# A scaled copy bound by its transfers: loads and stores in turns instead of side by side

## The chip, the cores and the metric

The kernel runs on one core of one Trainium2 chip. The metric is the device time of one execution in microseconds (us); lower is better. Engines are named as in the profile: DVE is VectorE, ACT is ScalarE, POOL is GpSimd, SP is SyncE. DVE and ACT do arithmetic here; SP and ACT also start DMA transfers, each through a queue of its own (q1 belongs to SP, q10 to ACT).

## The reference

Each of 16 x 1024 tokens has a row of 512 float32 numbers and two weights. The output holds the row twice, each copy multiplied by one of the token's weights. The expert indices are not used.

```python
batch, seq, hidden, n_experts = 16, 1024, 512, 8
k = 2
x_expanded = x[:, :, np.newaxis, :].repeat(k, axis=2)
weights = expert_weights[..., np.newaxis]
return (x_expanded * weights).astype(np.float32)
```

So 33.6 MB are read and 67.1 MB written.

## The kernel before, in words

The 16384 tokens are 128 partitions times 128 rows. They are cut into five tiles of 25 rows (row here: one token in each partition) and a rest of 3 rows. A tile's input is `x_tile` (two buffers in turn); its output is written into `o_ring`, which holds one tile's output of 25 rows and is used anew by each tile. The output is handled in two halves, rows 0 to 12 (13 rows, half A) and rows 13 to 24 (12 rows, half B). In each half DVE makes the products of the first 8 rows (9 in tile 0), four rows to an instruction, and ACT makes the others, one instruction for each output row of 512 numbers. Then SP issues the store of that half.

Loads are issued on ACT, stores on SP. Tile 0 is loaded in two pieces (9 and 16 rows), the others in one. The six loads of weights go first on SP's queue. The load of tile i+2 is issued when tile i has been multiplied, since it writes into tile i's buffer, and the rest `z_tile` is loaded with tile 2. The rest is multiplied and stored last. Nothing keeps loads and stores apart: a load goes as soon as its buffer is free, a store as soon as its half is multiplied, and a half is multiplied as soon as the store that read that half of `o_ring` before has landed. Each engine works through its own instructions in order; the semaphores between them are set by the framework from the data that they touch.

In the profile, L79 issues the loads of `x_tile`, L87 that of `z_tile`, L93 those of the weights, L106 is ACT's product, L116 DVE's product, L141 the store, and L76 a copy of one number that orders the load of the rest behind tile 0.

Of the kernel before, what the change touches and what calls it, by code (L numbers as in the profile page):

```python
# [1 line left out]

# [4 lines left out]


@with_exitstack
def kernel(  # L10
    ctx: ExitStack,
    tc: tile.TileContext,
    x: bass.AP,
    expert_indices: bass.AP,
    expert_weights: bass.AP,
    out: bass.AP,
):
    nc = tc.nc

    batch, seq, hidden = x.shape  # L20
    k = expert_weights.shape[-1]
    P = nc.NUM_PARTITIONS
    ntok = batch * seq
    assert ntok % P == 0
    A_TOTAL = ntok // P

    f32 = mybir.dt.float32
    row = k * hidden
    CH = 4


    groups = [25, 25, 25, 25, 25]
    TX = max(groups)
    LAST = 3
    FIRST = [9, 16]
    SHARES = [[9, 9], [8, 8]]
    assert sum(groups) + LAST == A_TOTAL

    xf = x.rearrange("b s h -> (b s) h")
    of = out.rearrange("b s k h -> (b s) (k h)")  # L40
    wf = expert_weights.rearrange("b s k -> (b s) k")

    w_pool = ctx.enter_context(tc.tile_pool(name="w_pool", bufs=1))
    x_pool = ctx.enter_context(tc.tile_pool(name="x_pool", bufs=2))
    o_pool = ctx.enter_context(tc.tile_pool(name="o_pool", bufs=1))

    w_tile = w_pool.tile([P, A_TOTAL * k], f32)
    o_ring = o_pool.tile([P, TX * row], f32)

    def rows(of_all, done, T):  # L50
        return of_all[done * P : (done + T) * P, :].rearrange(
            "(p a) n -> p (a n)", a=T
        )


    if LAST:
        z_pool = ctx.enter_context(tc.tile_pool(name="z_pool", bufs=1))
        z_tile = z_pool.tile([P, LAST * hidden], f32)

    tiles = []  # L60
    done = 0
    for n in groups:
        tiles.append((done, n))
        done += n

    loaded = []

    def load(i):
        if i >= len(tiles):
            return  # L70
        done, n = tiles[i]
        x_tile = x_pool.tile([P, TX * hidden], f32)
        src = rows(xf, done, n)
        steps = FIRST if i == 0 else [n]
        if i == 2 and LAST:
            nc.scalar.copy(out=z_tile[:, :1], in_=o_ring[:, TX * row - 1 :])  # L76
        for e, step in enumerate(steps):
            at = sum(steps[:e])
            nc.scalar.dma_start(  # L79
                out=x_tile[:, at * hidden : (at + step) * hidden],  # L80
                in_=src[:, at * hidden : (at + step) * hidden],
            )
            if i == 0 and e == 0:
                for g in range(len(tiles) + 1):
                    weights(g)
        if i == 2 and LAST:
            nc.scalar.dma_start(out=z_tile, in_=rows(xf, A_TOTAL - LAST, LAST))  # L87
        loaded.append(x_tile)


    def weights(e):
        at, n = tiles[e] if e < len(tiles) else (A_TOTAL - LAST, LAST)
        nc.sync.dma_start(  # L93
            out=w_tile[:, at * k : (at + n) * k], in_=rows(wf, at, n)
        )

    def product(engine, o_tile, t, x_in, c, m):

        o = t * row
        if engine is not None:  # L100
            for e in range(m * k):
                out_e = o_tile[:, o + e * hidden : o + (e + 1) * hidden]
                in_e = x_in[:, e // k * hidden : (e // k + 1) * hidden]
                w_e = w_tile[:, c + e : c + e + 1]
                if engine is nc.scalar or engine is nc.any and (c + e) % 3 == 2:
                    nc.scalar.mul(out=out_e, in_=in_e, mul=w_e)  # L106
                else:
                    nc.vector.tensor_scalar(
                        out=out_e,
                        in0=in_e,  # L110
                        scalar1=w_e,
                        scalar2=None,
                        op0=mybir.AluOpType.mult,
                    )
            return
        nc.vector.tensor_tensor(  # L116
            out=o_tile[:, o : o + m * row].rearrange(
                "p (t k h) -> p t k h", t=m, k=k
            ),
            in0=x_in[:, : m * hidden]  # L120
            .rearrange("p (t h) -> p t h", t=m)
            .unsqueeze(2)
            .to_broadcast([P, m, k, hidden]),
            in1=w_tile[:, c : c + m * k]
            .rearrange("p (t k) -> p t k", t=m)
            .unsqueeze(3)
            .to_broadcast([P, m, k, hidden]),
            op=mybir.AluOpType.mult,
        )

    def fill(o_tile, x_in, c, m, v):
        for t in range(0, v, CH):
            u = min(t + CH, v)
            product(None, o_tile, t, x_in[:, t * hidden : u * hidden], c + t * k, u - t)
        product(nc.scalar, o_tile, v, x_in[:, v * hidden :], c + v * k, m - v)

    def emit(src, dst, c, cuts, shares):
        for at, to, v in zip(cuts, cuts[1:], shares):
            o_tile = o_ring[:, at * row : to * row]
            fill(o_tile, src[:, at * hidden : to * hidden], c + at * k, to - at, v)  # L140
            nc.sync.dma_start(out=dst[:, at * row : to * row], in_=o_tile)  # L141

    for i in range(2):
        load(i)
    for i, (done, n) in enumerate(tiles):
        emit(loaded[i], rows(of, done, n), done * k, [0, 13, n], SHARES[min(i, 1)])
        load(i + 2)
    emit(
        z_tile,
        rows(of, A_TOTAL - LAST, LAST),  # L150
        (A_TOTAL - LAST) * k,
        [0, LAST],
        [LAST],
    )

# [1 line left out]
_INS = ['x', 'expert_indices', 'expert_weights']  # L157
_OUTS = [((16, 1024, 2, 512), 'float32')]


# [23 lines left out]
```

## Time and profile before

| | us |
|---|---|
| median of 3 runs | 239.59 (239.44 to 239.84) |
| profiled execution, its own time | 239.73 |
| its span, first to last instruction | 238.0 |
| DVE busy | 93.2 |
| ACT busy | 55.2 |
| POOL busy | 0.2 |

The span is what the profile's times count from; 1.73 us of the execution lie around it. The DMA figures of the profile are shares of the core's 16 DMA engines, so 100% means that all sixteen move data all the time. "To landing" is the time from the issue of a transfer until its semaphore says that all of it has arrived.

### The profile page before, as it was taken

The numbers are of one execution on the slowest core, as the hardware profiler recorded it, in microseconds if no ns is written. First come the engines' busy times: TensorE is split into PE (matmuls) and PEld (weight loads), VectorE is DVE, ScalarE is ACT, GpSimd is POOL, SyncE is SP. The second block draws the span as 40 slices with busy tenths as digits, with TensorE's granted clock in tenths as the row PEclk, the third lists the DMA queues.
The fourth block names the chain that finished last, engine by engine and source line by source line (L and its number), as shares of the span: only waits on it lengthen the run. The fifth ranks groups of instructions, "written<-read, shape, count | busy, mean of one in ns | idle before, by whom it ended". The sixth has DMA issues, their size and how long they took to land.

```text
span 238.0 us, 214 instructions
## 1 busy us (share of the span) xinstructions
DVE 93.2 (39%) x23; ACT 55.2 (23%) x88; POOL 0.2 (0%) x4
## 2 busy tenths in 40 slices
DVE  0599800000059193086005902920085292861300
ACT  0008800000054170081005302700080280800000
POOL 0000000000000000000000000000000000000000
DMA  6999999999999999999999999999999999999996
GB/s 252 445 415 493 475 415 414 415 386 457 430 406 397 434 439 456 458 430 415 405 435 484 430 434 434 413 405 431 490 430 448 417 397 423 457 448 438 438 397 264
DMA packets 3457, 100.80 MB, mean 424 GB/s; under 512 B 1152, under 2 KB 1152, under 8 KB 1280
## 3 DMA queue, kind: packets, MB, share of 16 engines
q1 hardware_dynamic: 2448, 67.24, 65.5%
q10 hardware_dynamic: 1008, 33.55, 33.1%
q14 instruction: 1, 0.01, 0.0%
HBM read 33.69 MB, written 67.11 MB: 424 GB/s over the span
## 4 chain that ended last, share of the span: by engine, by line
DMA 69%; DVE 16%; issue 5%; ACT 3%; ACTq 0%; DVEq 0%; SPq 0%
DMA out_dram<-o_ring 62%; DVE o_ring L116 16%; DMA x_tile<-in_x_dram 7%; ACT o_ring L106 2%; ACT L106 1%; ACTq L79 0%; DVEq L116 0%; SPq L141 0%; ACTq L106 0%
## 5 line engine op out<-in xcount | busy, mean ns | idle before, releaser
L116 DVE TENSOR_TENSOR o_ring<-x_tile,w_tile 128x4096 f32<-128x4096 f32 (+1 forms) x22 | 89.8, 4130 | 122.4 <-DMA out_dram<-o_ring 102.8
L106 ACT ACTIVATE o_ring<-x_tile,w_tile 128x512 f32<-128x512 f32 x86 | 53.7, 708 | 134.4 <-DMA out_dram<-o_ring 134.4
L116 DVE TENSOR_TENSOR o_ring<-z_tile,w_tile 128x3072 f32<-128x3072 f32 x1 | 3.4, 3359 | 7.0 <-DMA out_dram<-o_ring 7.0
L106 ACT ACT_TABLE_LOAD x1 | 1.3, 1283 | 18.8 <-DMA x_tile<-in_x_dram 18.8
L76 ACT COPY z_tile<-o_ring 128x1 f32<-128x1 f32 x1 | 0.2, 191 | 0.0
L168 POOL MEMSET const-bfloat16-1.0<- 128x1 bf16 x1 | 0.1, 102 | 0.0
L168 POOL MEMSET const-uint8-127<- 128x1 uint8 x1 | 0.1, 102 | 0.0
L168 POOL MEMSET const-float32-1.0<- 128x1 f32 x1 | 0.1, 99 | 0.0
L168 POOL MEMSET const-float32-0.0<- 128x1 f32 x1 | 0.1, 98 | 0.2 <-issue 0.2
## 6 DMA issues: line engine op xcount, KB each, us to landing
out_dram<-o_ring SPq DMA_DIRECT2D x5, 6656.0 KB, 32.7
out_dram<-o_ring SPq DMA_DIRECT2D x5, 6144.0 KB, 36.4
x_tile<-in_x_dram ACTq DMA_DIRECT2D x4, 6400.0 KB, 29.7
x_tile<-in_x_dram ACTq DMA_DIRECT2D x1, 4096.0 KB, 17.6
x_tile<-in_x_dram ACTq DMA_DIRECT2D x1, 2304.0 KB, 8.1
out_dram<-o_ring SPq DMA_DIRECT2D x1, 1536.0 KB, 14.6
z_tile<-in_x_dram ACTq DMA_DIRECT2D x1, 768.0 KB, 10.5
w_tile<-in_expert_weights_dram SPq DMA_DIRECT2D x5, 25.0 KB, 24.7
```

The source lines that it names most:

```text
L76: nc.scalar.copy(out=z_tile[:, :1], in_=o_ring[:, TX * row - 1 :])
L106: nc.scalar.mul(out=out_e, in_=in_e, mul=w_e)
L116: nc.vector.tensor_tensor(out=o_tile[:, o : o + m * row].rearrange("p (t k h) -> p t k h", t=m, k=k), in0=x_in[:, : m * hidden] .rearrange ...
L168: nc = _bacc.Bacc("TRN2", target_bir_lowering=False, num_devices=1)
```

## The change

Loads and stores are put into four turns: load tiles 0, 1, 2 and the rest; store tiles 0, 1 and the rest; load tiles 3 and 4; store tiles 2, 3 and 4. Two helpers make the turns out of copies of one or two numbers on POOL, which do no arithmetic that the output needs: a copy reads or writes what one side must have finished with and what the other side must wait for, and the framework's semaphores do the rest.

- `stores_wait(src)`: POOL copies two numbers out of the newly loaded tile into `hold`, then two numbers of `o_ring` (one in each half) into `hold`, and back. The stores of both halves come after that. It stands after the loads of tile 2 and of tile 4.
- `load_waits(dst, t)`: POOL copies a number of `o_ring`'s half B into `hold`, back (which must wait until the store of tile 1's half B has landed), and then into the tile that the load writes. It stands ahead of the load of tile 3.
- Something is left in the queue at each turn: tile 2 is loaded as 24 rows and 1 row and then the rest, and tile 4 as 21 and 4 rows, and the stores wait for the first piece only; the rest's store (3 rows) stands behind that of tile 1, and the load of tile 3 waits for tile 1's store only.

The rest is multiplied ahead of tile 2 into rows 10 to 12 of `o_ring`, no longer at the end. Only the weights of tile 0 stay on SP's queue; the others go in three DMAs on ACT's queue, behind the load of tile 1. In the built kernel ACT's queue has, ahead of the load of tile 3, one product of tile 2 that needs the landing of tile 1's half B; and the first DVE instruction of tile 2's half B (rows 17 to 20) waits for that same landing, while the second (rows 13 to 16) waits for POOL.

```diff
-    FIRST = [9, 16]
-    SHARES = [[9, 9], [8, 8]]
+    CUT = 13
+    STEPS = {0: [9, 16], 2: [24, 1], 4: [21, 4]}
...
+    def stores_wait(src):
+        held = o_ring[:, : CUT * row + 1 : CUT * row]
+        nc.gpsimd.tensor_copy(out=hold, in_=src[:, :2])
+        nc.gpsimd.tensor_copy(out=hold, in_=held)
+        nc.gpsimd.tensor_copy(out=held, in_=hold)
+
+    def load_waits(dst, t):
+        one = o_ring[:, t * row : t * row + 1]
+        nc.gpsimd.tensor_copy(out=hold[:, :1], in_=one)
+        nc.gpsimd.tensor_copy(out=one, in_=hold[:, :1])
+        nc.gpsimd.tensor_copy(out=dst[:, :1], in_=one)
+
+    load(0, 0)
+    weights(nc.sync, 0, 1)
+    load(0, 1)
+    load(1, 0)
+    weights(nc.scalar, 1, 3)
+    weights(nc.scalar, 3, 5)
+    nc.scalar.dma_start(
+        out=w_tile[:, (A_TOTAL - LAST) * k :], in_=rows(wf, A_TOTAL - LAST, LAST)
+    )
     for i, (done, n) in enumerate(tiles):
-        emit(loaded[i], rows(of, done, n), done * k, [0, 13, n], SHARES[min(i, 1)])
-        load(i + 2)
...
+        if i == 2:
+            at = CUT - LAST
+            product(None, o_ring, at, z_tile, (A_TOTAL - LAST) * k, LAST)
+            nc.sync.dma_start(
+                out=rows(of, A_TOTAL - LAST, LAST),
+                in_=o_ring[:, at * row : CUT * row],
+            )
+            load_waits(x_pair[1], CUT)
+            load(3, 0)
+            vector(src, c, 0, v)
+            vector(src, c, CUT, CUT + v)
+            scalar(src, c, CUT + v, n)
+            scalar(src, c, v, CUT)
+            load(4, 0)
+            nc.scalar.copy(
+                out=x_pair[0][:, STEPS[4][0] * hidden :][:, :1],
+                in_=o_ring[:, CUT * row - 1 : CUT * row],
+            )
+            load(4, 1)
+            stores_wait(x_pair[0])
+            store(dst, 0, CUT)
+            store(dst, CUT, n)
+            continue
+        for at, to in [(0, CUT), (CUT, n)]:
+            vector(src, c, at, at + v)
+            scalar(src, c, at + v, to)
+            if i > 0:
+                store(dst, at, to)
+        if i == 0:
+            nc.scalar.copy(out=z_tile[:, :1], in_=o_ring[:, TX * row - 1 :])
+            load(2, 0)
+            load(2, 1)
+            nc.scalar.dma_start(out=z_tile, in_=rows(xf, A_TOTAL - LAST, LAST))
+            stores_wait(x_pair[0])
+            store(dst, 0, CUT)
+            store(dst, CUT, n)
```

More of the change, by code (lines that the diff above doesn't have):

```diff
@@ L53, in rows @@
         )
-    if LAST:
-        z_pool = ctx.enter_context(tc.tile_pool(name="z_pool", bufs=1))
-        z_tile = z_pool.tile([P, LAST * hidden], f32)
     tiles = []
@@ L64, with load, weights @@
         done += n
[L66 to L94, printed above, removed]
+    def load(i, e):
+        at = sum(STEPS.get(i, groups[i : i + 1])[:e])
+        to = at + STEPS.get(i, groups[i : i + 1])[e]
+        part = slice(at * hidden, to * hidden)
+        nc.scalar.dma_start(out=x_pair[i % 2][:, part], in_=rows(xf, *tiles[i])[:, part])
+    def weights(engine, g, to):
+        at, n = tiles[g]
+        engine.dma_start(
+            out=w_tile[:, at * k : (at + (to - g) * n) * k].rearrange(
+                "p (g m) -> p g m", g=to - g
+            ),
+            in_=wf[at * P : (at + (to - g) * n) * P, :].rearrange(
+                "(g p a) n -> p g (a n)", g=to - g, p=P
+            ),
         )
@@ L129, in product @@
         )
[L131 to L141, printed above, removed]
@@ L143, with vector @@
-    for i in range(2):
-        load(i)
-    for i, (done, n) in enumerate(tiles):
-        emit(loaded[i], rows(of, done, n), done * k, [0, 13, n], SHARES[min(i, 1)])
-        load(i + 2)
[L148 to L154, printed above, removed]
+    def vector(src, c, at, to):
+        for t in range(at, to, CH):
+            u = min(t + CH, to)
+            product(
+                None, o_ring, t, src[:, t * hidden : u * hidden], c + t * k, u - t
+            )
@@ new lines @@
+    for i, (done, n) in enumerate(tiles):
+        src, dst, c = x_pair[i % 2], rows(of, done, n), done * k
+        v = 9 if i == 0 else 8
+        if i == 2:
+            at = CUT - LAST
+            product(
+                None, o_ring, at, z_tile, (A_TOTAL - LAST) * k, LAST
+            )
+            nc.sync.dma_start(
+                out=rows(of, A_TOTAL - LAST, LAST),
+                in_=o_ring[:, at * row : CUT * row],
+            )
+            load_waits(x_pair[1], CUT)
[8 more added lines that the diff above has]
+                in_=o_ring[:, CUT * row - 1 : CUT * row],
+            )
+            load(4, 1)
[16 more added lines that the diff above has]
+            store(dst, CUT, n)
```

10 lines of the change are left out of this document (9 added, 1 removed).

## The prediction

> **What bounds the kernel now.** I read the DMA queues first, then the stretches, then the chain.
>
> ```profile
> span 238.0 us, 214 instructions
> q1 hardware_dynamic: 2448, 67.24, 65.5%
> q10 hardware_dynamic: 1008, 33.55, 33.1%
> DMA 69%; DVE 16%; issue 5%; ACT 3%; ACTq 0%; DVEq 0%; SPq 0%
> ...
> core 0: us, DVE busy (x) ACT busy (x) POOL busy (x), PEclk, DMA share, GB/s
> 0.00:1.80 1.80, 0.00 (x0) 0.00 (x0) 0.20 (x4) 1.00 0.02 3
> 5.00:48.00 43.00, 19.73 (x6) 10.16 (x16) 0.00 (x0) 1.00 1.01 432
> 52.00:92.00 40.00, 17.52 (x4) 11.24 (x18) 0.00 (x0) 1.00 1.00 434
> 96.00:122.00 26.00, 8.76 (x2) 6.24 (x10) 0.00 (x0) 1.00 1.00 435
> 100.00:168.00 68.00, 26.28 (x6) 17.48 (x28) 0.00 (x0) 1.00 1.00 431
> 236.90:238.00 1.10, 0.00 (x0) 0.00 (x0) 0.00 (x0) 1.00 0.00 0
> ```
>
> The queues' packets take 65.5 + 33.1 = 98.6% of the time of all sixteen DMA engines. What is missing is 1.4% of 238.0, or 3.3 us, and 1.8 us of that lie before the first packet and 1.1 us behind the last. So 0.4 us of idle DMA time are left in the whole middle. The chain says 69% DMA and gives 16% to DVE, but DVE's time costs nothing as long as the queues stay full, and the DMA share stands at 1.00 in the stretches where DVE multiplies. The bound is the transfers.
>
> Next, are loads and stores slower side by side? These stretches must first be told apart:
>
> ```profile
> ## 3 DMA queue, kind: packets, MB, share of 16 engines
> q10 hardware_dynamic: 497, 18.50, 99.6%
> q1 hardware_dynamic: 497, 0.09, 1.1%
> ...
> q1 hardware_dynamic: 409, 18.31, 58.7%
> q10 hardware_dynamic: 263, 12.65, 40.7%
> ...
> 25.12 42.86 DMA out_dram<-o_ring
> ```
>
> The first pair of rows is the stretch from 5 to 48 us: only loads (q10), with the weights in q1. The first store, issued at 25.12, lands 42.86 us later, at 67.98: on q1 it stands behind the weights, whose small pieces pass one by one between the loads' large ones, so loads of tiles 0, 1, 2 and the rest are over at about 51 before a store moves. From 52 to 92 there are only stores (the next load is issued at 91.41, below). The second pair is 96 to 168: both mixed. The rates are 432 alone, 434 alone, 435 and 431 mixed. Mixing costs nothing that could be won: (1 - 431/434) of 68 us is 0.5 us, and with the 0.4 us of gaps 0.9 us is the most that turns can bring. And the first turn is there already; what is new is the second half.
>
> **The change part by part.** Durations that I need:
>
> ```profile
> out_dram<-o_ring SPq DMA_DIRECT2D x5, 6656.0 KB, 32.7
> out_dram<-o_ring SPq DMA_DIRECT2D x5, 6144.0 KB, 36.4
> x_tile<-in_x_dram ACTq DMA_DIRECT2D x4, 6400.0 KB, 29.7
> out_dram<-o_ring SPq DMA_DIRECT2D x1, 1536.0 KB, 14.6
> z_tile<-in_x_dram ACTq DMA_DIRECT2D x1, 768.0 KB, 10.5
> ...
> L141 SPq DMA_DIRECT2D out_dram<-o_ring x11: 332/333/348, 25.1 to 222.5; - x11
> ...
> L116 DVE TENSOR_TENSOR o_ring<-x_tile,w_tile 128x4096 f32<-128x4096 f32 x20 | 87.6, 4421 | 122.4 <-DMA out_dram<-o_ring 102.8 <-issue 10.7 <-DMA x_tile<-in_x_dram 8.9
> L106 ACT ACTIVATE o_ring<-x_tile,w_tile 128x512 f32<-128x512 f32 x86 | 53.7, 708 | 134.4 <-DMA out_dram<-o_ring 134.4
> L116 DVE TENSOR_TENSOR o_ring<-z_tile,w_tile 128x3072 f32<-128x3072 f32 x1 | 3.4, 3359 | 7.0 <-DMA out_dram<-o_ring 7.0
> L76 ACT COPY z_tile<-o_ring 128x1 f32<-128x1 f32 x1 | 0.2, 191 | 0.0
> L168 POOL MEMSET const-bfloat16-1.0<- 128x1 bf16 x1 | 0.1, 102 | 0.0
> ...
> 0.73 8.50 ACTq L79 DMA_DIRECT2D x_tile<-in_x_dram  x3
> 91.41 0.36 ACTq L79 DMA_DIRECT2D x_tile<-in_x_dram  x1
> ...
> 219.00 0.03 issue
> 219.03 0.05 DVEq L116
> 219.08 0.04 issue
> 219.12 3.36 DVE o_ring L116
> ```
>
> At 434 GB/s (KB are 1024 bytes) half A's store streams for 15.7 us, half B's for 14.5, the rest's for 3.6; at 432 a tile loads in 15.2, the rest in 1.8, four rows in 2.4. Three small times: issue to first packet on an idle queue is 1.1 us (issued at 0.73, nothing before 1.80); last packet to landing is 0.3 us (the last store, issued at 222.5, lands 14.6 later at 237.1, and nothing moves after 236.9); landing to start of the waiting instruction is 0.12 us (219.00 to 219.12).
>
> Bytes are the same: no change in transfer time. Five tiles of weights move from q1 to q10 behind tile 1. On q1 they took 1.1% of 43 us, 0.5 us; on q10 I take the same, from nothing to twice that. They are needed first at 67, by tile 1. Two loads are split in two, which adds eight pieces to each DMA engine for each split, at most 0.1 us.
>
> *Turn 1, loads to stores, at about 51 us.* SP's first store now waits for POOL, and all stores queue behind it. The wait ends with the landing of tile 2's 24 rows, when one row (0.6) and the rest (1.8), 2.4 us, are still to stream. The path beside it: landing 0.3, three POOL copies one behind the other, 1.1 to the first packet. That leaves 1.0 us for the copies. A copy is 0.10 (POOL's MEMSET) to 0.19 (ACT's COPY of one column) plus 0.12 for its wait, so three take 0.7 to 0.9 us. Covered, cost 0 (0.6 if a copy takes 0.5 with its wait). DVE is idle then: tile 0 is multiplied by 28.7, and tile 1 must wait for the first store.
>
> *Inside the stores' turns.* A half's products start when the store before last lands: 0.3 + 0.12 + two DVE instructions of 4.42 + 1.1 to the first packet is 10.4 us, beside a 14.5 us store of the other half. Covered by 4 us, as from 52 to 92 now. If that cover went, each us over it would be lost.
>
> *Turn 2, stores to loads, at about 112.* Stores of tiles 0 and 1 take 2 x (15.7 + 14.5) = 60.4 us from 51, and the rest's store goes to 115.4. ACT's load of tile 3 waits for POOL; behind it on ACT queue the other products of tile 2 and the load of tile 4. It is released by the landing of tile 1's half B; what covers it is the rest's store, 3.6 us. The path: landing 0.3, two POOL copies 0.6 (on ACT one product of 0.71 and its wait, beside them: 0.8), first packet 1.1, together 2.2. That would be covered. But the same landing releases a DVE instruction of 4.42 us (rows 17 to 20), which reads two tiles, and DVE is free at that moment: the rest's product (3.36) and two of 4.42 begin at 98 and end at about 110. So the two POOL copies start beside it. No instant of the trace has POOL beside a working DVE: its four MEMSETs are over before the first packet. The price of the second copy is therefore open between 0.19 and 4.42 + 0.19 us. I take the upper end: a forecast shouldn't spend an overlap that no row shows, where two engines are let go by one event, and the longer instruction is the nearest row for how long the shorter may be held. Then the path is 0.3 + 0.12 + 4.42 + 0.19 + 0.12 + 1.1 = 6.2 us against a cover of 3.6, and sixteen DMA engines stand idle for **2.6 us**. At the lower end it costs 0.
>
> The Trainium skill, "SBUF — State Buffer", section on engine ports, says that VectorE's second input comes through a read port shared with GpSimd, so that a VectorE instruction with two SBUF inputs and a GpSimd instruction that reads SBUF exclude each other for a whole instruction. No run here shows it yet; by it turn 2 would cost those 2.6 us, without it nothing.
>
> Who waits then: DVE's next instruction (rows 13 to 16) needs POOL's last copy, and was to start at that time anyway. ACT has 13 products left (13 x 0.71 = 9.2 us) ahead of tile 4's load, which is thus issued at about 127, while tile 3 streams until 133. Covered by some 5 us.
>
> *Turn 3, loads to stores, at about 148.* As turn 1: four rows (2.4 us) cover 0.3 + 0.9 + 1.1. DVE is idle (tile 2 is done by 122). Cost 0 to 0.2, taken as 0.
>
> *The end.* The rest's product and store leave the end, where the product (219.12 to 222.48) lay beside half B's store. The last transfer is now half B of 12 rows. No change.
>
> Sum against the profiled execution: 239.73 + 2.6 = 242.3. The median of the three runs stands 0.14 below that execution, so 242.2.
>
> **The rivals.** *Nothing is held (not slower).* POOL's copies pass beside DVE, and each turn is covered. It decides at turn 2: as long as load 3's first packet comes within 3.6 us of the last packet of tile 1's store, that is, copies within 2.2 us of the landing, nothing is lost. For it: the 2.2 us path in total above. Against: the one DVE instruction beside it. Time: 239.6, between 239.2 and 240.3 with the splits, the weights and a visible 0.2 to 0.5 at turns 1 and 3.
>
> *Turns bring something.* Separate directions save the 0.9 us bounded above: 238.7. Against it stand 432, 434 and 435. For it only the 0.4 us of gaps and a mean of 431 in the long mixed stretch.
>
> *Every turn shows.* POOL's copies, none of which the trace has, take some 0.7 us each with their waits, not 0.3. Then turns 1 and 3 each stick out by 3 x 0.4 = 1.2 us, less 0.1, and turn 2 stays covered: 241.8; with the hold at turn 2, 244.8.
>
> *The change doesn't do what it says.* Turn 1 is such a case already: loads came first anyhow, so the wait there changes nothing by itself. For tiles 3 and 4 the semaphores leave no way round.
>
> **How the numbers follow.** Hold at turn 2: 0.50, 242.2, its own range 241.6 to 242.9. Nothing held: 0.28. Turns bring something: 0.08. Every turn shows: 0.14. About 0.2%, 0.5 us, is what a measurement of this kernel can tell from no change. Of "nothing held" 0.20 fall within that, 0.05 above and 0.03 below. So faster 0.11, same 0.20, slower 0.69. For 8 in 10 the range must reach down to 239.3, into "nothing held", and up to 243.3, over the hold's own range with a little for turns 1 and 3.
>
> **What would show it.** In the trace after: POOL's third copy of the load's wait starts over 4 us after the store of tile 1's half B lands, at the end of a 4.42 us DVE instruction, and the DMA share has one hole of 2 to 3 us between 112 and 120. At about 51 and 148 no hole over 0.3 us. Stretches of pure loads and pure stores stay at 432 and 434. It is wrong if POOL's copies run while DVE works (time near 239.6), if holes stand at 51 and 148, or if a pure stretch runs above 436.

## The result: 1.6% slower, and the profile after

The changed kernel takes 243.42 us (median of 6 runs, 243.22 to 243.45) against 239.62 for the kernel before (6 runs, 239.44 to 239.84): a ratio of 1.0157, 95% interval 1.0144 to 1.0170. That is 3.80 us more. The forecast had 242.2, 2.6 us more, and 243.42 lies 0.12 us above the top of its range.

The page of the changed kernel, the rows that answer to those of before:

```profile
span 241.6 us, 235 instructions
DVE 93.1 (39%) x23; ACT 55.4 (23%) x89; POOL 10.2 (4%) x13
...
q1 hardware_dynamic: 1728, 67.14, 64.5%
q10 hardware_dynamic: 1984, 33.66, 33.0%
...
L141 POOL COPY hold<-o_ring 128x1 f32<-128x1 f32 x1 | 4.3, 4252 | 36.6 <-DVE o_ring L100 36.6
L142 POOL COPY o_ring<-hold 128x1 f32<-128x1 f32 x1 | 4.4, 4421 | 21.4 <-DMA out_dram<-o_ring 21.4
L135 POOL COPY hold<-o_ring 128x2 f32<-128x2 f32 x2 | 0.4, 186 | 0.1
```

The queues' packets fill 97.5% of the DMA time in place of 98.6%. POOL's copies of one or two numbers come in two sorts: 0.19 us, and 4.25 and 4.42 us. The timeline says what the long ones have beside them. First the two long copies, the second of them at turn 2, then turn 1:

```profile
81.92 8.76 DVE L100 TENSOR_TENSOR o_ring<-x,w_tile 128x4096 f32<-128x4096 f32 x2 [5.63 <-DMA out_dram<-o_ring]
86.48 4.25 POOL L141 COPY hold<-o_ring 128x1 f32<-128x1 f32 x1 [36.55 <-DVE o_ring L100]
...
112.12 4.42 DVE L100 TENSOR_TENSOR o_ring<-x,w_tile 128x4096 f32<-128x4096 f32 x1 [2.39 <-DMA out_dram<-o_ring]
112.17 4.42 POOL L142 COPY o_ring<-hold 128x1 f32<-128x1 f32 x1 [21.44 <-DMA out_dram<-o_ring]
116.66 0.18 POOL L143 COPY x<-o_ring 128x1 f32<-128x1 f32 x1
116.87 0.33 ACTq L68 DMA_DIRECT2D x<-in_x_dram  x1
116.87 4.42 DVE L100 TENSOR_TENSOR o_ring<-x,w_tile 128x4096 f32<-128x4096 f32 x1 [0.33 <-POOL x L143]
...
49.25 0.18 POOL L134 COPY hold<-x 128x2 f32<-128x2 f32 x1 [48.81 <-DMA x<-in_x_dram]
49.49 0.18 POOL L135 COPY hold<-o_ring 128x2 f32<-128x2 f32 x1
49.74 0.19 POOL L136 COPY o_ring<-hold 128x2 f32<-128x2 f32 x1
49.95 41.12 SPq L127 DMA_DIRECT2D out_dram<-o_ring  x4
```

The copy at 86.48 ends at 90.73, just behind VectorE's pair of instructions (90.68). It cost nothing, since the next copy had to wait for the landing at 112.03 anyway. At turn 2 one landing releases VectorE at 112.12 and POOL at 112.17. POOL's copy of one number lasts as long as VectorE's instruction. The next copy passes at once, since VectorE's next instruction must wait for POOL. Tile 3's load is issued at 116.87. At turn 1, where VectorE is idle, the three copies pass in 0.7 us. The stretches around turn 2 (columns as before: busy time of DVE, ACT and POOL, clock, DMA share, GB/s):

```profile
111.00:115.30 4.30, 3.18 (x1) 0.72 (x1) 3.13 (x1) 1.00 0.86 366
115.30:117.80 2.50, 2.17 (x2) 0.55 (x1) 1.48 (x2) 1.00 0.00 0
117.80:120.00 2.20, 2.20 (x1) 2.20 (x5) 0.00 (x0) 1.00 1.22 372
```

From 115.3 to 117.8 no DMA engine moves anything: the rest's store is done and the load hasn't begun. In the whole hole, its edges included, 2.79 us of sixteen engines are lost.

The rest of the difference I took from the DMA packet records of the two traces: the time in which fewer than sixteen pieces run, and the time of the pieces themselves (a piece is what one partition sends or gets in one transfer; a transfer has 128, eight on each DMA engine). In us of sixteen engines:

| | before | after | difference |
|---|---|---|---|
| idle at turn 2 | 0 | 2.79 | +2.79 |
| idle at turns 1 and 3 | 0.12 | 0.22 + 0.25 | +0.35 |
| idle at the start and the end | 2.33 + 0.47 | 2.14 + 0.20 | -0.46 |
| pieces of tile 3's load (mean 1.895 and 1.994 us each) | 15.16 | 15.95 | +0.79 |
| pieces of all stores of 12 and 13 rows | 151.25 | 151.82 | +0.57 |
| pieces of the rest's load (mean 0.314 and 0.241 us each) | 2.51 | 1.93 | -0.58 |
| all other pieces | 65.72 | 65.99 | +0.27 |
| sum | | | +3.7 |

The spans differ by 3.6 us, the medians by 3.8. In the prediction's terms: the third copy started 4.6 us after the landing, the hole at turn 2 is there, and no hole over 0.3 us stands at 51 or 148.

### The profile page after: what moved, and what is told of

The parts are those of the page before. It is cut to its first block, busy times and chain, and to the rows that moved or that the text cites. A ratio compares the mean times of both kernels' runs of the same rounds, so it can differ in the third digit from the quotient of the medians.

```text
span 241.6 us, 235 instructions
## 1 busy us (share of the span) xinstructions
DVE 93.1 (39%) x23; ACT 55.4 (23%) x89; POOL 10.2 (4%) x13
## 4 chain that ended last, share of the span: by engine, by line
DMA 55%; DVE 15%; issue 13%; ACT 3%; POOL 2%; DVEq 2%; SPq 0%; ACTq 0%; POOLq 0%
DMA out_dram<-o_ring 44%; DVE o_ring L100 15%; DMA x<-in_x_dram 12%; ACT o_ring L90 3%; POOL o_ring L142 2%; DVEq L221 2%; SPq L127 0%; POOL hold L134 0%; POOL hold L135 0%; ACTq L68 0%; POOLq L221 0%; POOL o_ring L136 0%; POOL x L143 0%; DVEq L100 0%; POOLq L136 0%
## 5 line engine op out<-in xcount | busy, mean ns | idle before, releaser
L100 DVE TENSOR_TENSOR o_ring<-x,w_tile 128x4096 f32<-128x4096 f32 (+1 forms) x22 | 89.9, 4130 | 119.2 <-DMA out_dram<-o_ring 109.8
L90 ACT ACTIVATE o_ring<-x,w_tile 128x512 f32<-128x512 f32 x86 | 53.8, 708 | 140.5 <-DMA out_dram<-o_ring 125.3
L141 POOL COPY hold<-o_ring 128x1 f32<-128x1 f32 x1 | 4.3, 4252 | 36.6 <-DVE o_ring L100 36.6
L142 POOL COPY o_ring<-hold 128x1 f32<-128x1 f32 x1 | 4.4, 4421 | 21.4 <-DMA out_dram<-o_ring 21.4
```

What stands on the lines that cost most here:

```text
L100: nc.vector.tensor_tensor(out=o_tile[:, o : o + m * row].rearrange("p (t k h) -> p t k h", t=m, k=k), in0=x_in[:, : m * hidden] .rearrange ...
L141: nc.gpsimd.tensor_copy(out=hold[:, :1], in_=one)
L142: nc.gpsimd.tensor_copy(out=one, in_=hold[:, :1])
```

## The experiments

Theory 1: POOL's reading copy is shut out for as long as a VectorE instruction with two inputs in SBUF runs, and this hold makes the hole. Theory 2: POOL is late after a DMA landing whatever it does and whatever runs beside it. Theory 3: turning from stores to loads costs in itself. All times are medians with the ratio to the kernel before from the same runs.

**No POOL read beside VectorE.**

```diff
-        nc.gpsimd.tensor_copy(out=hold[:, :1], in_=one)
-        nc.gpsimd.tensor_copy(out=one, in_=hold[:, :1])
-        nc.gpsimd.tensor_copy(out=dst[:, :1], in_=one)
+        nc.gpsimd.memset(one, 0.0)
+        nc.scalar.copy(out=dst[:, :1], in_=one)
```

> As the changed kernel, but the wait ahead of tile 3's load has no POOL instruction that reads: POOL sets the number in half B of o_ring (a write, which waits for the landing of tile 1's half B), and ACT copies it into the load's tile. VectorE's 4.42 us instruction still starts at the same landing. Theory 1 (the hold is a POOL read beside a VectorE instruction with two inputs): POOL's instruction takes 0.1 us, no hole between 112 and 120, the first pieces of tile 3's load take their usual 1.89 us; the 2.8 us of idle DMA and some 0.8 us of slow first pieces go: 239.7 to 240.2. Theory 2 (POOL is late after a DMA landing whatever it does): POOL's instruction still ends over 4 us after the landing, 243.4. Theory 3 (turning from stores to loads costs in itself): the hole goes but the first pieces stay slow, 240.4 to 241.0.

Measured: 240.53 us, 1.0031 (1.0019 to 1.0043). Its timeline:

```profile
112.03 8.76 DVE L100 TENSOR_TENSOR o_ring<-x,w_tile 128x4096 f32<-128x4096 f32 x2 [2.39 <-DMA out_dram<-o_ring]
112.07 0.10 POOL L141 MEMSET o_ring<- 128x1 f32 x1 [62.23 <-DMA out_dram<-o_ring]
112.64 0.17 ACT L142 COPY x<-o_ring 128x1 f32<-128x1 f32 x1
112.85 0.33 ACTq L68 DMA_DIRECT2D x<-in_x_dram  x1
```

POOL starts 0.04 us after VectorE and is done in 0.10 us: a write isn't held. The load is issued 4 us sooner and the hole is gone. That speaks against theory 2, though a write isn't a copy; VectorE let go after POOL, below, settles it for copies. The time lies at theory 3's lower end, so something is left over: the first pieces of tile 3's load didn't come down to the 1.89 us that I had expected, but to 2.23 on average, and the rest's store took 0.35 us more.

**VectorE's instruction cut in half.**

```diff
-    def vector(src, c, at, to):
-        for t in range(at, to, CH):
-            u = min(t + CH, to)
+    def vector(src, c, at, to, ch=CH):
+        for t in range(at, to, ch):
+            u = min(t + ch, to)
...
-            vector(src, c, CUT, CUT + v)
+            vector(src, c, CUT, CUT + v, 2)
```

> As the changed kernel, but VectorE multiplies half B of tile 2 in instructions of two rows (2.2 us) instead of four (4.42 us). Theory 1: POOL's copy L142 lasts as long as the VectorE instruction beside it, about 2.2 us; the hole shrinks from 2.8 to about 0.6 us and the slow first pieces shrink or stay: 240.4 to 241.3. Theory 2: POOL's copy keeps its 4.4 us, 243.4. Theory 3: as theory 1, at the upper end.

Measured: 241.23 us, 1.0069 (1.0057 to 1.0081).

```profile
111.92 2.29 DVE L100 TENSOR_TENSOR o_ring<-x,w_tile 128x2048 f32<-128x2048 f32 x1 [2.41 <-DMA out_dram<-o_ring]
111.98 2.29 POOL L142 COPY o_ring<-hold 128x1 f32<-128x1 f32 x1 [21.48 <-DMA out_dram<-o_ring]
114.33 0.18 POOL L143 COPY x<-o_ring 128x1 f32<-128x1 f32 x1
114.54 0.33 ACTq L68 DMA_DIRECT2D x<-in_x_dram  x1
```

The copy follows the instruction beside it, 2.29 and 2.29 us. The copy is 2.13 us shorter than in the changed kernel, and the hole shrinks by 2.10, to 0.69 us by the packet records. This is theory 1 with its size.

**VectorE let go after POOL.** POOL still reads, and touches one number of each of the two VectorE instructions, so that neither can start before it.

```diff
-        one = o_ring[:, t * row : t * row + 1]
-        nc.gpsimd.tensor_copy(out=hold[:, :1], in_=one)
-        nc.gpsimd.tensor_copy(out=one, in_=hold[:, :1])
-        nc.gpsimd.tensor_copy(out=dst[:, :1], in_=one)
+        one = o_ring[:, t * row : (t + CH) * row + 1 : CH * row]
+        nc.gpsimd.tensor_copy(out=hold, in_=one)
+        nc.gpsimd.tensor_copy(out=one, in_=hold)
+        nc.gpsimd.tensor_copy(out=dst[:, :2], in_=one)
```

> As the changed kernel, but POOL's copies of the load's wait touch one number of each of VectorE's two instructions of tile 2's half B, so that VectorE can't start either before POOL is done. Nothing else moves, and POOL still reads. Theory 1: POOL's copies take 0.19 us each, VectorE starts 0.5 us later than now, which costs nothing; no hole: 239.7 to 240.2. Theory 2: 243.4. Theory 3: 240.4 to 241.0.

Measured: 240.31 us, 1.0028 (1.0019 to 1.0036).

```profile
111.93 0.19 POOL L142 COPY o_ring<-hold 128x2 f32<-128x2 f32 x1 [21.23 <-DMA out_dram<-o_ring]
112.17 0.18 POOL L143 COPY x<-o_ring 128x2 f32<-128x2 f32 x1
112.39 0.33 ACTq L68 DMA_DIRECT2D x<-in_x_dram  x1
112.39 8.76 DVE L100 TENSOR_TENSOR o_ring<-x,w_tile 128x4096 f32<-128x4096 f32 x2 [2.92 <-POOL x L143]
```

The same reads take 0.19 us right behind the landing once VectorE stands still, and theory 2 is out. With this the hold is shown from three sides: by what POOL does, by the length of its neighbour, and by their order. That it needs a VectorE instruction with two inputs isn't shown: no run here has one with a single input beside a copy of POOL's. The hold cost 243.42 - 240.31 = 3.1 us, of which 2.8 are the hole. But 0.6 us over the kernel before are left without any hole at turn 2, between the 239.7 to 240.2 that theory 1 gave and the 240.4 of theory 3. The packet records show where: the load's first pieces now meet the last pieces of the rest's store, whose 128 pieces take 0.54 us on average in place of 0.46, 0.64 us of sixteen engines together; and the stores of 12 and 13 rows keep their 0.57 us. Against that the rest's load is 0.58 shorter, as in the changed kernel.

**The kernel before with the weights moved.** Only tile 0's weights stay on SP's queue; no other edit.

```diff
-                for g in range(len(tiles) + 1):
-                    weights(g)
+                weights(nc.sync, 0)
+        if i == 1:
+            for g in range(1, len(tiles) + 1):
+                weights(nc.scalar, g)
...
-    def weights(e):
+    def weights(engine, e):
...
-        nc.sync.dma_start(
+        engine.dma_start(
```

> The kernel before, with one part of the change: only tile 0's weights stay on SP's queue, the others go on ACT's queue behind the load of tile 1. So the first store no longer stands behind the weights and starts at about 26, beside the loads of tiles 1 and 2: no turn at all is left. If mixing costs nothing, as the rates of 432, 434 and 435 say, 239.2 to 239.8. If the turn that the weights made by accident was worth something, above 240.

Measured: 241.41 us (240.88 to 243.68), 1.0072 (1.0052 to 1.0091). So the turn that the weights made by accident was worth 1.7 us, if their new place costs nothing by itself; the run with longer leftovers, below, has them on ACT's queue too and takes 239.51. Two stretches of its profiled execution, which at 243.68 is the longest of the six:

```profile
92.00:140.00 48.00, 17.52 (x4) 11.24 (x18) 0.00 (x0) 1.00 1.01 436
236.00:240.80 4.80, 0.00 (x0) 0.00 (x0) 0.00 (x0) 1.00 0.22 92
```

In the middle the queues are as full as ever. Tile 1's products now wait for their weights until 56.2, but the DMA share from 30 to 66 is 1.01, so that isn't the loss either. In this execution the loss is at the end, where some DMA engines have nothing left and others still have two pieces to go: 3.5 us of sixteen engines are idle there. Stores that start amid the first loads bring the engines apart, by 3.3 us at the first store, and a transfer ends with its slowest engine. The pieces of tile 1's load also took 2.05 us each where 1.89 is usual.

**The first turn alone.** Turns 2 and 3 are taken out: the loads of tiles 3 and 4 go as in the kernel before, and the rest comes last.

```diff
-    STEPS = {0: [9, 16], 2: [24, 1], 4: [21, 4]}
+    STEPS = {0: [9, 16], 2: [24, 1]}
...
-        if i == 2:
...
-            load_waits(x_pair[1], CUT)
-            load(3, 0)
...
-            stores_wait(x_pair[0])
...
+        elif i < 3:
+            load(i + 2, 0)
+    product(None, o_ring, 0, z_tile, (A_TOTAL - LAST) * k, LAST)
+    store(rows(of, A_TOTAL - LAST, LAST), 0, LAST)
```

> Of the change only the first turn and the weights' place are kept: stores wait for the loads of tile 2, then the loads of tiles 3 and 4 go as in the kernel before, as soon as their buffer is free, and the rest comes last. If all of the change's loss lies at turns 2 and 3 and mixing costs nothing from there on: 239.2 to 239.9. If starting to mix makes the sixteen DMA engines drift apart, as it did when only the weights were moved (241.41, engines ending up to 4 us apart), part of that comes back: 240.3 to 241.5.

Measured: 241.81 us, 1.0083 (1.0071 to 1.0095): slower than with all three turns and no hold (240.31). There is no hole in the middle; the loss is in the pieces, at the start of tile 3's load beside tile 1's store. In the kernel before this start is free. One thing in which the two differ is how far apart the sixteen DMA engines run. It can be read from the spread of the starts of a store's first sixteen pieces:

| from the packet records | spread, us | mean store piece of 53,248 bytes, us | mean piece of tile 3's load, us |
|---|---|---|---|
| before, tile 1's half A | 0.99 | 1.966 | 1.895 |
| first turn alone | 0.23 | 2.142 | 1.996 |
| first turn, longer leftovers (below) | 0.48 | 1.967 | 1.978 |

**Longer leftovers.** From the run with VectorE after POOL; the stores are let go while more is still to load.

```diff
-    STEPS = {0: [9, 16], 2: [24, 1], 4: [21, 4]}
+    STEPS = {0: [9, 16], 2: [22, 3], 4: [19, 6]}
```

> As the run in which VectorE starts after POOL (240.31), but with more left in the queue when the stores are released at turns 1 and 3: tile 2 is loaded as 22 and 3 rows, tile 4 as 19 and 6, 3.6 us of loads in place of 2.4. The holes at turns 1 and 3 (0.2 us together in that run) go: 240.0 to 240.2. If the turns cost by themselves, no change: 240.3.

Measured: 239.51 us, 0.9984 (0.9976 to 0.9993): a little faster than the kernel before, and the best of all. All the turns are still there, so they cost nothing by themselves, and theory 3 is out. The time went below the 240.0 that the holes alone explain. The holes at turns 1 and 3 are gone, and besides, the engines leave turn 1 0.66 us apart in place of 0.33, the store pieces are back at 1.966 to 1.969 us, and the rest's store at 0.460. Its queues:

```profile
span 237.8 us, 235 instructions
q1 hardware_dynamic: 1728, 67.14, 65.3%
q10 hardware_dynamic: 1984, 33.66, 33.3%
```

98.6% again, as before the change.

**Still longer leftovers.**

```diff
-    STEPS = {0: [9, 16], 2: [22, 3], 4: [19, 6]}
+    STEPS = {0: [9, 16], 2: [20, 5], 4: [17, 8]}
```

> As the run with longer leftovers (239.51), with 20 and 5 rows of tile 2 and 17 and 8 of tile 4, so 4.9 us of loads left at each release. Holes at the turns are gone already, so by the holes alone nothing changes: 239.3 to 239.7. If more loads beside the first stores spread the engines further and that saves more: 239.0 to 239.3; if it costs at the end of the span, above 239.7.

Measured: 241.27 us (239.76 to 241.78), 1.0057 (1.0040 to 1.0074). In the profiled execution, which at 241.78 is the longest of the twelve, the engines leave turn 3 2.1 us apart, one piece, and keep that to the end:

```profile
235.00:238.80 3.80, 0.00 (x0) 0.00 (x0) 0.00 (x0) 1.00 0.15 65
```

At the end 2.4 us of sixteen engines are lost, where the kernel before lost 0.47. Two of the twelve runs took 239.76 and 239.92; how far apart the engines were in those isn't recorded. Of the three sizes tried, 2.4, 3.6 and 4.9 us, the middle one is the best: the shortest left small holes and engines nearly in step, and with the longest the engines came apart.

**The first turn with longer leftovers.**

```diff
-    STEPS = {0: [9, 16], 2: [24, 1]}
+    STEPS = {0: [9, 16], 2: [22, 3]}
```

> As the run with the first turn only (241.81), but tile 2 is loaded as 22 and 3 rows, so that stores start while loads still stream and the sixteen DMA engines leave the turn 0.7 us apart in place of 0.2 to 0.4. Theory A (a load that starts beside stores is slow when the engines run in step, and free when they are apart, as in the kernel before with 1.0 us): the 2.2 us of slow pieces at the start of tile 3's load shrink to 0.5 us or less, 239.7 to 240.3. Theory B (starting to mix costs whatever the engines' phase): 241.4 to 241.9.

Measured: 240.55 us (240.01 to 243.08), 1.0045 (1.0025 to 1.0066). The profiled execution took 240.06. The slow pieces at the start of tile 3's load went from 2.2 to 0.7 us (table above), with the engines 0.48 us apart in place of 0.23. That speaks for theory A. So does the pair of runs with the release at half A, below: slow pieces beside the load's start come to 1.9 us with the engines 0.31 us apart, and to 0.5 with 0.61. It isn't clean: in both pairs the spread came with the longer leftovers, and here the time lies a little above the range given. The cause stays open.

**Leftovers with the hold left in.**

On the changed kernel itself:

```diff
-    STEPS = {0: [9, 16], 2: [24, 1], 4: [21, 4]}
+    STEPS = {0: [9, 16], 2: [22, 3], 4: [19, 6]}
```

> The changed kernel with the longer leftovers alone (22 and 3, 19 and 6 rows); POOL's copy is still held by VectorE at turn 2. Theory 1: the hole at turn 2 stays at 2.8 us with some 0.8 us of slow first pieces of the load; the holes at turns 1 and 3 (0.5 us together) and the slightly slow store pieces (0.6 us) go: 242.2 to 242.8. If leftovers heal the whole, 239.5.

Measured: 242.86 us, 1.0128 (1.0115 to 1.0141); a hole of 3.1 us at turn 2, none at turns 1 and 3. The leftovers don't heal the hold; against the longer leftovers without it the difference is 3.35 us, a second measure of what the hold costs.

**Release at half A.**

```diff
-            load_waits(x_pair[1], CUT)
+            load_waits(x_pair[1], 0)
```

> As the changed kernel, but the load of tile 3 waits for the landing of tile 1's half A in place of half B (load_waits gets row 0 in place of row 13). POOL's copy then starts beside VectorE's product of the rest. Theory 1: it is held for those 3.4 us just the same, but 14.5 us of store are left to cover it: no hole. The load starts beside large store pieces, as in the kernel before. If the slow first pieces come from starting beside small pieces or from rest, they go too: 239.5 to 240.0. If they come with every start of a load after stores, 240.2 to 240.6.

Measured: 248.01 us, 1.0339 (1.0326 to 1.0352). Both cases that I had given are wrong, and the timeline says why:

```profile
97.32 0.19 POOL L142 COPY o_ring<-hold 128x1 f32<-128x1 f32 x1 [21.38 <-DMA out_dram<-o_ring]
97.37 3.36 DVE L100 TENSOR_TENSOR o_ring<-z_tile,w_tile 128x3072 f32<-128x3072 f32 x1 [7.07 <-DMA out_dram<-o_ring]
97.57 3.20 POOL L143 COPY x<-o_ring 128x1 f32<-128x1 f32 x1
100.80 0.34 ACTq L68 DMA_DIRECT2D x<-in_x_dram  x1
121.83 8.76 DVE L100 TENSOR_TENSOR o_ring<-x,w_tile 128x4096 f32<-128x4096 f32 x2 [12.27 <-DMA out_dram<-o_ring]
133.20 3.78 ACT L90 ACTIVATE o_ring<-x,w_tile 128x512 f32<-128x512 f32 x6 [4.59 <-DMA out_dram<-o_ring]
137.01 0.33 ACTq L68 DMA_DIRECT2D x<-in_x_dram  x1
...
131.00:138.00 7.00, 0.00 (x0) 3.97 (x7) 0.00 (x0) 1.00 0.19 68
```

The hold itself is as theory 1 says: the copy that started 0.05 us ahead of VectorE took 0.19, the next was held for 3.20 us, to the end of VectorE's instruction, and cost nothing under a long store. But the load then shares the DMA engines with tile 1's half B and the rest's store. Half B lands at 121.8 in place of 112, the rest at 133.2, and ACT's last products of tile 2 wait for that. Tile 4's load waits for those products and is issued at 137.01; tile 3 has been loaded since 130.5. From 131 to 138 the DMA share is 0.19. A transfer let in earlier took the time of the transfer on whose landing the next one depends.

**Both together.**

```diff
-    STEPS = {0: [9, 16], 2: [24, 1], 4: [21, 4]}
+    STEPS = {0: [9, 16], 2: [22, 3], 4: [19, 6]}
...
-            load_waits(x_pair[1], CUT)
+            load_waits(x_pair[1], 0)
```

> Both of the last two edits together: release at half A, and 3.6 us of loads left at turns 1 and 3. What is left then is the turns as such with no hole: 239.3 to 239.8 if the edits add; not under 238.9, since the transfers' own time is the same as before.

Measured: 247.08 us (246.21 to 249.02), 1.0321 (1.0288 to 1.0355). A hole of the same kind, 6.1 us of sixteen engines where release at half A alone has 6.3; the edits don't add, since the first makes a new wait.

## Why the prediction was right and wrong

**The hold at turn 2, the step that the forecast stood on, was right** in mechanism and place: one copy as long as the VectorE instruction beside it, one hole between 112 and 120. The reading copy was held for 4.42, 2.29 and 3.20 us, and the instruction that only writes took 0.10 us beside VectorE. The section "Who interferes with whom" of the Trainium skill's page "SBUF — State Buffer" says that a VectorE instruction with two SBUF inputs contends with a GpSimd instruction that reads SBUF and not with one that only writes it, and the traces agree. The prediction's "exclude each other" is seen in one direction only: where POOL's copy came first by 0.05 us (release at half A), VectorE's product took its usual 3.36 us. The term was put at 2.6 us and measured 2.79. The path was 116.87 - 112.03 = 4.8 us from the landing to the issue, as worked out, but the engines got their first piece 0.96 to 1.55 us after the issue, and I had taken 1.1 for all.

**What made it wrong is the sum, which put three terms at nothing.** First, the start of tile 3's load had no price: its first piece on each engine took 2.3 to 3.1 us in place of 1.89, 0.79 us in all. The rows that I had, 432 and 435 GB/s, are means over tens of us and can't show a start. Second, turn 1 ("Covered, cost 0") and turn 3 ("taken as 0") cost 0.22 + 0.25. The three POOL copies took 0.7 us as estimated; what I had left out is that the landing is that of the slowest engine, and at turn 1 the sixteen engines land from 48.24 to 49.11. The early ones have less than my 2.4 us left to stream when it comes. Third, "Bytes are the same: no change in transfer time" failed for the stores: their pieces took 0.57 us more, and why is open. Against these 1.83 us stand 0.58 won back in the rest's load, which no longer meets the weights, and 0.46 at the start and the end. The sum had neither, so that it missed by only 1.2 us is in part luck.

Two slips of the working change nothing: by its own terms the rest's store ends at 115.0 and not 115.4 (51 + 60.4 + 3.6; it ended at 115.3), and copies of 0.5 us would stick out at turn 1 by 0.5, not 0.6.

**"Mixing costs nothing" was true of the trace that it was read from and false as a rule.** The kernel before mixes from 92 us on at full rate, with engines 1.0 us apart. The same mixing cost 2.2 us in the run with the first turn alone, and mixing from the first store on cost 1.7 us when only the weights were moved. I had noted that the first turn was there by accident and drew from it that the new wait changes nothing; that this accident earned its keep I hadn't seen.

**The rivals.** "Nothing held" at 239.6 was measured by letting VectorE go after POOL: 240.31, for the missing terms above. "Turns bring something", given 0.08: the kernel with longer leftovers is faster than the kernel before, by 0.16% with an interval that ends at 0.07%, but not for that rival's reason. Its stores' pieces take 151.36 us of sixteen engines where the kernel before has 151.25, so they are no faster alone than mixed; shorter is the rest's load, 1.91 in place of 2.51, without the weights beside it. "Every turn shows" was wrong in its price: a POOL copy and its wait took 0.24 us, not 0.7.

The covers inside the stores' turns and ACT's cover ahead of tile 4's load held: the load was issued at 125.35, with tile 3 streaming to 134.6.

## What to carry to other kernels

A wait made of a small POOL copy lasts as long as the VectorE product that it meets: here 4.42 us in place of 0.19. Let VectorE start after the copy, or use an instruction that doesn't read; both took the hole away. When transfers take turns, the cover at a turn must count from the DMA engine that is done first; here 2.4 us were too short, and with 4.9 us the engines came apart. Before a load is let in earlier, look at which landing the load after it depends on.

## What the runs showed of the hardware that was not expected

- A load that starts from rest has slow first pieces. In the changed kernel they took 2.28 to 3.06 us on the sixteen engines, where the later ones take 1.89; at the start of tile 4's load in the run with the release at half A, 2.32 on average where the later ones take 1.59. When the load starts beside the small last pieces of a store, some of these are slowed (up to 0.91 us for 0.46), and the load's first pieces take 1.94 us (VectorE let go after POOL) or 2.23 (no POOL read).
- In these runs DMA engines nearly in step are slightly slow. Stores take 1.970 to 1.977 us on average for a piece of 53,248 bytes where the engines are about 0.5 us apart or less and no load starts beside them; they take 1.966 to 1.969 where the engines are 0.53 us or more apart, with two exceptions: in the run with two-row products the stores after turn 3 were 0.62 us apart and still took 1.972 to 1.976, and the last 13-row store in the run with both edits, 1.2 us apart, took 1.970. Why is open; no run changed the spread alone.
- Small transfers ahead of a large one on the same queue hold it up for long while another queue streams. With six loads of weights (128 KB together) ahead on its queue, the first store of the kernel before got its first piece 25.8 us after its issue (25.12 to 50.94); with one ahead, in the run with the weights moved, 5.3 us (24.84 to 30.09). Loads streamed beside it in both.
